# The low part of split weights: a VectorE subtraction, or an adding transfer onto a negated high part

## The chip, the cores and the metric

The kernel runs on one core of a Trainium2 chip. The metric is the device time of one execution in microseconds. Before the change, three timed runs took 3363.51, 3373.67 and 3374.84 us, median 3373.67. One more execution was taken by the hardware profiler; durations below are from it. A core has TensorE (matmuls), VectorE, ScalarE and GpSimd (elementwise work), and SyncE, which only issues transfers. SyncE and GpSimd each have a queue of transfers, issued in program order.

## The reference, cut to what matters

Two stacked blocks on a sequence of 512 positions with 1024 features, all in float32. The first block has two layers; each is a gated feed-forward net, a hybrid mixer (causal attention with a decay, beside a depthwise causal convolution), a second feed-forward net and a gated addition. The second block has four layers of different kinds: a state-space mixer, sliding-window attention, attention over a compressed latent, and a gated unit that mixes positions.

```python
for i in range(DEPTH):                       # first block, 2 layers
    h = h + 0.5 * swiglu(rmsnorm(h, g_ff1[i]), w_ff1_in[i], w_ff1_out[i])
    h = h + hybrid_mixer(rmsnorm(h, g_mix[i]), w_in[i], ...)
    h = h + 0.5 * swiglu(rmsnorm(h, g_ff2[i]), w_ff2_in[i], w_ff2_out[i])
    h = h + sigmoid(rmsnorm(h, g_ple[i]) @ w_ple_gate[i]) * (p[i] @ w_ple_proj[i])
...
for i in range(4):                           # second block: s5, swa, mla, sgu
    x = x + rmsnorm(branch_i(rmsnorm(x, pre_norm[i])), post_norm[i])
```

## The kernel before, in words

Each product of two float32 matrices is done as three matmuls in a reduced-precision float format (`mm3`, L445 to 451). Both operands are split into a high part, the value rounded to that format, and a low part, the value less its high part; the three matmuls are high by high, high by low and low by high, all added up in one PSUM bank.

Weights are packed on the host into units of 8 blocks of 128x128, that is 128x1024 floats or 512 KB. A unit goes through three steps, all called from `block`, by way of `_advance` and `_ahead`:

- `_dma` (L385): SyncE loads the unit from HBM into a `raw` buffer, of which there are 3.
- `_split` (L393): ScalarE casts `raw` to the high part `whi` (L406), and VectorE subtracts it from `raw` to give the low part `wlo` (L407; in the profile its line is L248, that of a helper which records every VectorE operation). `whi` and `wlo` have 3 buffers each.
- the matmuls: eight blocks, three matmuls each.

When the program comes to unit i, it has recorded the split of units up to i+2 and loads for some units more. `self.ui` is then i. There is no scheduler behind that: instructions stand on each engine in the order in which the Python code records them, and each engine works through its own in order. A unit marked `keep` is split into slots of another pool instead; these are the output weights of the four layers of the second block.

The units come in the order of the phases. A first-block layer has 66 units for the first feed-forward net, 52 for the mixer, 66 for the second net and 10 for the gated addition. The second block has 24 units of input weights for the state-space layer (`s5w`), 18 for the sliding window (`swaw`), 33 for the latent attention (`mlaw`), 24 for the gated unit (`sguw`), and 8 kept ones behind each.

GpSimd has other work in the stages that the change touches: scaling rows of attention scores (L1059, L1767), sums of squares (L651), loads of tables for the state-space layer (L1532), loads of a bias table (L1662) and of constants (L1857, L2008). SyncE's queue also carries rearranging copies between partitions, such as those of keys (L951), among the loads of weights.

Of the kernel before, what the change touches and what calls it, by code (L numbers as in the profile page):

```python
# [9 lines left out]
F32R = mybir.dt.float32r  # L10
I32 = mybir.dt.int32
AF = mybir.ActivationFunctionType
ALU = mybir.AluOpType
# [278 lines left out]
class Kern:  # L292
# [84 lines left out]
        return self.vt[:, o + j:o + j + n]  # L377


    def add_units(self, name, keep=False):  # L380
        a = self.t[name]
        for u in range(a.shape[0]):
            self.units.append((a[u], keep))

    def _dma(self):  # L385
        i = self.dmai
# [6 lines left out]
    def _split(self):  # L393
        i = self.spli
        r = self.raws.pop(i)
        if self.units[i][1]:
            hl = self.slots(2), self.slots(2)
            self.kept.append(hl)
        else:
            hl = [[self.wp.tile([P, UB * P], F32, tag=n, name=self.nm(n))] for n in ("whi", "wlo")]  # L400
        self.sps[i] = self.r(hl)
        self.spli += 1
        w = UB * P // len(hl[0])

        def piece(hi, lo, src):
            self.nc.scalar.copy(hi.bitcast(F32R), src)  # L406
            self.v.tensor_tensor(lo.bitcast(F32R), src, hi, op=ALU.subtract)  # L407
        if i == 0:
            a, b = slice(0, w // 2), slice(w // 2, w)
            piece(hl[0][0][:, a], hl[1][0][:, a], r[:, a])  # L410
            return lambda: piece(hl[0][0][:, b], hl[1][0][:, b], r[:, b])
        for j, (hi, lo) in enumerate(zip(*hl)):
            piece(hi, lo, r[:, j * w:(j + 1) * w])
# [1723 lines left out]
def run(tc, t, outT, phases):  # L2137
    with ExitStack() as ctx:
        k = Kern(ctx, tc, t, outT)
        with tc.manual_schedule():  # L2140
            for ph in phases:
                for u in ph[1]:
                    k.add_units(u, ph[0] in ("s5", "swa", "mla", "sgu") and u[-1] == "o")
            k.load()
            k.first(phases[0][2])
            if any(ph[0] in ("s5", "swa") for ph in phases):
                k.aux = Paced(k, k.prepare(), TABLE_RATE)
                if phases[0][0] != "ffn":
                    k.aux.finish()
                    k.aux = None  # L2150
            for i, ph in enumerate(phases):
                nxt = phases[i + 1][2] if i + 1 < len(phases) else (None, 0)
                getattr(k, ph[0])(*ph[3:], nxt)
            if phases[-1][0] != "sgu":
                k.final_out()
# [34 lines left out]
```

## Time and profile before

| | us |
|---|---|
| timed runs, median (lowest to highest) | 3373.67 (3363.51 to 3374.84) |
| profiled execution | 3365.56 |
| its span, first to last instruction | 3363.8 |
| TensorE busy | 3227.5 |
| VectorE busy | 2136.9 |
| ScalarE busy | 1315.8 |
| GpSimd busy | 454.5 |

In the rows below PE is TensorE, PEld its loading of weights, DVE VectorE, ACT ScalarE, POOL GpSimd and SP SyncE. A name such as `wlo<-raw,whi` gives what an instruction writes and reads, without buffer numbers. An arrow in brackets behind a row gives the idle time of the engine before it and what ended that time. Stretches of the span: the first mixer from about 350 to 704 us, the second from about 1480 to 1835, the state-space layer from 2285, the sliding window from 2535, the latent attention from 2770 and the gated unit from 3105 to the end.

### The profile page before, as it was taken

Reading aid. Unit: us, or ns where it says so; the run is one execution under the profiler, and the core shown is the slowest. Engines: PE = TensorE matmul, PEld = TensorE weight load, DVE = VectorE, ACT = ScalarE, POOL = GpSimd, SP = SyncE. Lnnn points to the kernel's source line nnn. Section 1 sums busy time; section 2 is a strip of 40 time slices with the busy share of each in tenths; the row PEclk is TensorE's granted clock in tenths of the full one; section 3 lists DMA queues with packets and bytes.
Section 4 is the critical chain, followed back from the end, with each engine's and each line's share of the span. In section 5 each row is a group of like instructions: output and inputs, shape, how many; then the busy total and the mean of one; then the engine's idle time right before and its main releaser. Section 6 shows DMA issues by size and latency. Waiting matters only on the chain. (4 is left out here: it accounts for less than half of the span.)

```text
span 3363.8 us, 42316 instructions
## 1 busy us (share of the span) xinstructions
PE 3227.5 (96%) x15704; PEld 2704.2 (80%) x15704; DVE 2136.9 (64%) x4128; ACT 1315.8 (39%) x2250; POOL 454.5 (14%) x582
## 2 busy tenths in 40 slices
PE   9999999999999999999999999999999989998997
PEld 7888777788888888887777888887888778787887
DVE  6653488866653676536887654347766766587665
ACT  4322335433322333323444333234334664466433
POOL 0100013001100011000120000010303332044201
PEclk9999999999999999999999999999899989999998
DMA  5433232224432234332322332343732122322221
GB/s 178 137 108 101 88 113 70 92 90 132 139 121 95 94 129 138 114 99 93 99 72 94 104 119 94 106 138 108 257 95 92 63 63 76 110 73 62 86 83 63
DMA packets 122862, 352.27 MB, mean 105 GB/s; under 512 B 31072, under 2 KB 33792, under 8 KB 122656
## 3 DMA queue, kind: packets, MB, share of 16 engines
q1 hardware_dynamic: 106384, 299.88, 28.3%
q0 software_dynamic: 16272, 49.69, 4.4%
q8 instruction: 124, 2.03, 0.2%
q14 instruction: 82, 0.67, 0.1%
HBM read 312.75 MB, written 28.11 MB: 101 GB/s over the span
## 5 line engine op out<-in xcount | busy, mean ns | idle before, releaser
L449 PE MATMUL mm<-s,whi 128*128 128x512 f32 (+1 forms) x3528 | 1382.0, 392 | 20.9 <-DVE s L248 9.1
L451 PE MATMUL mm<-s,wlo 128*128 128x512 f32 (+1 forms) x3528 | 1367.1, 388 | 6.2 <-DVE wlo L248 6.2
L450 PE MATMUL mm<-s,whi 128*128 128x512 f32 (+1 forms) x3528 | 1368.2, 388 | 3.4 <-DVE s L248 3.0
L248 DVE TENSOR_TENSOR wlo<-raw,whi 128x1024 fp32r<-128x1024 f32 (+1 forms) x488 | 594.3, 1224 | 522.9 <-ACT whi L406 519.0
L449 PEld LDWEIGHTS mm<-s,whi 128*128 128x128 f32 x3528 | 667.9, 189 | 153.0 <-ACT s L740 7.4
L451 PEld LDWEIGHTS mm<-s,wlo 128*128 128x128 f32 x3528 | 667.1, 189 | 145.6 <-DVE wlo L248 10.2
L450 PEld LDWEIGHTS mm<-s,whi 128*128 128x128 f32 x3528 | 667.9, 189 | 135.4 <-DVE s L248 8.1
L406 ACT CAST whi<-raw 128x1024 fp32r<-128x1024 f32 (+1 forms) x488 | 508.3, 1046 | 552.1 <-PE mm L450 271.2
L248 DVE TENSOR_TENSOR s<-s,s 128x512 f32<-128x512 f32 (+10 forms) x944 | 471.7, 524 | 170.7 <-ACT s L595 140.7
L248 DVE TENSOR_TENSOR s<-mm,rbc 128x512 f32<-128x512 f32 x296 | 199.4, 685 | 177.7 <-PE mm L451 156.7
L595 ACT CAST s<-s 128x512 fp32r<-128x512 f32 (+1 forms) x213 | 129.9, 616 | 401.2 <-DVE s L248 397.3
L1059 POOL TENSOR_SCALAR s<-s,m 128x128 f32<-128x128 f32 (+3 forms) x128 | 154.5, 1213 | 501.5 <-DVE m L248 388.4
L248 DVE SCALAR_TENSOR_TENSOR s<-s,vecs,s 128x511 f32<-128x511 f32 (+13 forms) x256 | 183.9, 759 | 10.4 <-ACT s L598 6.9
L457 PE MATMUL sd<-s,s 128*128 128x256 f32 (+2 forms) x624 | 125.8, 327 | 40.1 <-DVE s L248 22.8
L457 PEld LDWEIGHTS sd<-s,s 128*128 128x128 f32 x624 | 105.7, 199 | 65.9 <-DVE s L248 33.2
L449 PE MATMUL mm<-s,s 128*128 128x256 f32 x448 | 132.2, 295 | 26.6 <-ACT s L595 22.7
L847 ACT ACTIVATE s<-s 128x512 f32<-128x512 f32 x88 | 55.7, 632 | 253.2 <-DVE s L248 253.2
L740 ACT ACTIVATE s<-h,vecs 128x512 fp32r<-128x512 f32 (+1 forms) x112 | 70.8, 633 | 182.5 <-DVE h L248 182.5
L450 PE MATMUL mm<-s,s 128*128 128x256 f32 x448 | 130.7, 292 | 1.9 <-DVE s L248 1.3
L451 PE MATMUL mm<-s,s 128*128 128x256 f32 x448 | 129.7, 289 | 0.8 <-DVE s L248 0.8
L248 DVE SCALAR_TENSOR_TENSOR s<-h,vecs,s 128x512 fp32r<-128x512 f32 (+1 forms) x112 | 81.2, 728 | 66.9 <-ACT s L740 66.9
L449 PE MATMUL sd<-s,whi 128*128 128x512 f32 x296 | 122.0, 412 | 0.9 <-ACT whi L406 0.9
(213 smaller groups left out, 3264.6 us busy)
## 6 DMA issues: line engine op xcount, KB each, us to landing
raw<-in_mix_dram SPq DMA_DIRECT2D x104, 512.0 KB, 3.5
raw<-in_ff2i_dram SPq DMA_DIRECT2D x88, 512.0 KB, 3.5
raw<-in_ff1i_dram SPq DMA_DIRECT2D x87, 512.0 KB, 3.6
raw<-in_ff1o_dram SPq DMA_DIRECT2D x44, 512.0 KB, 3.5
raw<-in_ff2o_dram SPq DMA_DIRECT2D x44, 512.0 KB, 3.5
raw<-in_mlaw_dram SPq DMA_DIRECT2D x33, 512.0 KB, 3.5
tab<-s POOLq DMA_DIRECT2D x64, 256.0 KB, 2.3
s<-tab POOLq DMA_DIRECT2D x64, 256.0 KB, 6.1
```

Of the source, the lines that this page charges most:

```text
L248: return f(*a, **kw)
L406: self.nc.scalar.copy(hi.bitcast(F32R), src)
L449: mm(ps, wh, xh, start=first, stop=False)
L450: mm(ps, wh, xl, start=False, stop=False)
L451: mm(ps, wl, xh, start=False, stop=last)
L457: self.nc.tensor.matmul(ps, w, x[j], start=first and j == 0, stop=last and j == 1)
L595: nc.scalar.copy(hi.bitcast(F32R), src)
L740: self.nc.scalar.activation(hi.bitcast(F32R), src, AF.Copy, scale=gv)
L847: nc.scalar.activation(sg, ta, AF.Silu)
L1059: nc.gpsimd.tensor_scalar(out=pr[:, c], in0=pr[:, c], scalar1=ri, scalar2=None, op0=ALU.mult)
```

## The change

Units of the mixers and of the second block's input weights get their low part in another way. ScalarE writes the negated, rounded raw weights into `wlo` (an activation with scale -1), and then a transfer on GpSimd's queue, from SBUF to SBUF, adds the raw weights onto it. The sum is again raw less high part. Units of the feed-forward nets and of the gated addition, kept units, and units that are split no more than one ahead of the unit being started (`i > self.ui + 1` is false) still use the subtraction.

```diff
--- before.py
+++ after.py
@@ -377,10 +377,10 @@
         return self.vt[:, o + j:o + j + n]
 
 
-    def add_units(self, name, keep=False):
+    def add_units(self, name, keep=False, summed=False):
         a = self.t[name]
         for u in range(a.shape[0]):
-            self.units.append((a[u], keep))
+            self.units.append((a[u], keep, summed and not keep))
 
     def _dma(self):
         i = self.dmai
@@ -402,9 +402,17 @@
         self.spli += 1
         w = UB * P // len(hl[0])
 
+
+
+        summed = self.units[i][2] and i > self.ui + 1
+
         def piece(hi, lo, src):
             self.nc.scalar.copy(hi.bitcast(F32R), src)
-            self.v.tensor_tensor(lo.bitcast(F32R), src, hi, op=ALU.subtract)
+            if summed:
+                self.nc.scalar.activation(lo.bitcast(F32R), src, AF.Copy, scale=-1.0)
+                self.nc.gpsimd.dma_start(lo, src, accum_op=ALU.add)
+            else:
+                self.v.tensor_tensor(lo.bitcast(F32R), src, hi, op=ALU.subtract)
         if i == 0:
             a, b = slice(0, w // 2), slice(w // 2, w)
             piece(hl[0][0][:, a], hl[1][0][:, a], r[:, a])
@@ -2140,7 +2148,7 @@
         with tc.manual_schedule():
             for ph in phases:
                 for u in ph[1]:
-                    k.add_units(u, ph[0] in ("s5", "swa", "mla", "sgu") and u[-1] == "o")
+                    k.add_units(u, ph[0] in ("s5", "swa", "mla", "sgu") and u[-1] == "o", ph[0] not in ("ffn", "ple"))
             k.load()
             k.first(phases[0][2])
             if any(ph[0] in ("s5", "swa") for ph in phases):
```

In the order of instructions 188 low parts move. On ScalarE, at the end of the first mixer, where casts of weights stand among casts of the mixer's own tiles (`raw` is a loaded unit, `s` a slot), before:

```order
L406 CAST whi_5367<-raw_5244 128x1024
L1007 CAST s_5385<-s_4911 128x512
L1007 CAST s_5404<-s_4949 128x512
L406 CAST whi_5411<-raw_5290 128x1024
L1007 CAST s_5429<-s_4988 128x512
L1007 CAST s_5448<-s_5026 128x512
L406 CAST whi_5455<-raw_5328 128x1024
```

And now:

```order
L410 CAST whi_5409<-raw_5284 128x1024
L412 ACTIVATE wlo_5410<-raw_5284 128x1024
L1015 CAST s_5428<-s_4943 128x512
L1015 CAST s_5447<-s_4982 128x512
L410 CAST whi_5454<-raw_5331 128x1024
L412 ACTIVATE wlo_5455<-raw_5331 128x1024
L1015 CAST s_5473<-s_5022 128x512
L1015 CAST s_5492<-s_5061 128x512
L410 CAST whi_5499<-raw_5370 128x1024
```

Lines in the changed file are 4 or 8 higher. Each cast of a unit is followed by a second pass over the same raw tile, and the mixer's casts stand behind both.

On GpSimd, in the sliding-window layer, where the bias table is loaded into slots and sums of squares follow, before:

```order
L1662 DMA s_19873<-bias_d 128x2x256
L1662 DMA s_19874<-bias_d 128x2x256
L1662 DMA s_19875<-bias_d 128x2x256
L1662 DMA s_19876<-bias_d 128x2x256
L651 TENSOR_TENSOR s_19736<-s_19736,s_19991 128x256
L651 TENSOR_TENSOR s_19736<-s_19736,s_19998 128x256
```

And now:

```order
L1670 DMA s_19994<-bias_d 128x2x256
L1670 DMA s_19995<-bias_d 128x2x256
L1670 DMA s_19996<-bias_d 128x2x256
L1670 DMA s_19997<-bias_d 128x2x256
L413 DMA wlo_20022<-raw_19562 128x1024
L659 TENSOR_TENSOR s_19857<-s_19857,s_20113 128x256
L659 TENSOR_TENSOR s_19857<-s_19857,s_20120 128x256
```

The adding transfer stands behind the last bias load and ahead of the sums. It waits for ScalarE's second pass, and so do the sums behind it.

## Rows read from the trace of the kernel before

**Rows 1.** Page head and section 1: busy time, share and instructions of each engine

```profile
span 3363.8 us, 42316 instructions
PE 3227.5 (96%) x15704; PEld 2704.2 (80%) x15704; DVE 2136.9 (64%) x4128; ACT 1315.8 (39%) x2250; POOL 454.5 (14%) x582
```

**Rows 2.** Stretches: length, busy of PE, PEld, DVE, ACT, POOL, clock, DMA, GB/s

```profile
350.00:704.00 354.00, 332.57 (x1492) 269.85 (x1491) 266.32 (x511) 147.73 (x244) 43.97 (x38) 0.98 0.29 88
704.00:1065.00 361.00, 360.59 (x1628) 298.75 (x1627) 213.99 (x381) 119.17 (x160) 29.75 (x56) 1.00 0.37 121
2535.00:2770.00 235.00, 206.68 (x1249) 183.09 (x1248) 166.97 (x454) 131.20 (x373) 83.15 (x97) 0.94 0.20 66
```

**Rows 3.** Waits of TensorE: us in total, times, longest us

```profile
PE sd L457 <- DVE s L248: 22.8, 22, 4.3
PE mm L449 <- DVE s L248: 10.5, 9, 2.1
```

**Rows 4.** Page section 5: costliest groups, the weight split

```profile
L248 DVE TENSOR_TENSOR wlo<-raw,whi 128x1024 fp32r<-128x1024 f32 (+1 forms) x488 | 594.3, 1224 | 522.9 <-ACT whi L406 519.0
L406 ACT CAST whi<-raw 128x1024 fp32r<-128x1024 f32 (+1 forms) x488 | 508.3, 1046 | 552.1 <-PE mm L450 271.2
```

**Rows 5.** Transfers: queue's share; issues, count, size, us to landing

```profile
q1 hardware_dynamic: 106384, 299.88, 28.3%
raw<-in_mix_dram SPq DMA_DIRECT2D x104, 512.0 KB, 3.5
s<-in_wsT_dram POOLq DMA_DIRECT2D x4, 256.0 KB, 4.6
tab<-s POOLq DMA_DIRECT2D x64, 256.0 KB, 2.3
bias_d<-bias POOLq DMA_DIRECT2D x1, 3072.0 KB, 14.6
```

**Rows 6.** Timeline, undisturbed stretch: start, us, engine, instruction, idle before

```profile
595.66 1.05 ACT L406 CAST whi<-raw 128x1024 fp32r<-128x1024 f32 x1 [1.13 <-PE mm L450]
607.02 0.39 PE L451 MATMUL mm<-s,wlo 128*128 128x512 f32 x1
```

**Rows 7.** Timeline, first mixer: late splits and VectorE's chain

```profile
404.12 1.98 ACT L406 CAST whi<-raw 128x1024 fp32r<-128x1024 f32 x2
407.34 0.50 PE L451 MATMUL mm<-s,wlo 128*128 128x512 f32 x1 [1.40 <-DVE wlo L248]
675.58 1.23 DVE L248 TENSOR_TENSOR wlo<-raw,whi 128x1024 fp32r<-128x1024 f32 x1 [1.64 <-ACT whi L406]
712.87 1.04 ACT L406 CAST whi<-raw 128x1024 fp32r<-128x1024 f32 x1
716.73 0.39 PE L451 MATMUL mm<-s,wlo 128*128 128x512 f32 x1
```

**Rows 8.** Timeline, start of the state-space stage

```profile
2303.91 1.04 ACT L406 CAST whi<-raw 128x1024 fp32r<-128x1024 f32 x1
2306.26 0.50 PE L451 MATMUL mm<-s,wlo 128*128 128x512 f32 x1 [0.53 <-DVE wlo L248]
```

**Rows 9.** Timeline, last late split, in the gating stage

```profile
3277.89 1.04 ACT L406 CAST whi<-raw 128x1024 fp32r<-128x1024 f32 x1
3282.46 0.39 PE L451 MATMUL mm<-s,wlo 128*128 128x512 f32 x1
```

**Rows 10.** Timeline, sliding-window stage, GpSimd's bias loads

```profile
2564.59 5.04 POOL L1662 DMA_DIRECT2D s<-bias_d  x7
2569.09 0.28 PE L451 MATMUL mm<-s,wlo 128*128 128x256 f32 x1
```

**Rows 11.** Timeline, first mixer, SyncE's queue and the cast before

```profile
436.46 1.05 ACT L406 CAST whi<-raw 128x1024 fp32r<-128x1024 f32 x1
439.12 0.33 SPq L389 DMA_DIRECT2D raw<-in_mix_dram  x1
441.68 2.50 SPq L951 DMA_DIRECT2D s<-s  x4
```

## The prediction

> **What bounds the kernel now.** I read the busy shares first, then the busy time by stage, then who waits for whom on TensorE, and last the timelines around the weight splits. TensorE is busy in 3227.5 of 3363.8 us [rows 1], so an edit on another engine counts only where it makes TensorE start earlier or later. The stages differ [rows 2]: in the feed-forward stretch TensorE is busy 360.59 of 361 us, in the first mixer 332.57 of 354 (the second is its like), in the sliding-window stage 206.68 of 235 at a granted clock of 0.94. The change leaves the feed-forward and gate weights as they are, so all that it can win lies in the stages that have gaps.
>
> What ends those gaps: 22.8 us of waits for VectorE results before the attention products and 10.5 us before projections [rows 3]. That is the part that a less loaded VectorE could shorten, 33.3 us in all.
>
> What stands against it is how early a weight unit is split. In the undisturbed stretch a unit's high part is cast as soon as TensorE has let go of its buffer: the cast at 595.66 was released by a matmul and ended at 596.71, and the first matmul on this unit's low part (the third of its first block) starts at 607.02 [rows 6]. That is 10.3 us from the cast's end to the first use, two units' worth of matmuls. I call this the margin. Before, one VectorE subtraction of 1.22 us had to fit in it.
>
> **The change part by part.** The order shows 188 low parts that leave VectorE, 188 activations that come to ScalarE and 188 transfers that come to GpSimd's queue. Per unit:
>
> VectorE loses 1224 ns, 188 x 1.224 = 230 us. It also loses the wait for the cast ahead of it: 519 us over 488 units, 1.06 us each [rows 4]. Since VectorE works in order, whatever stood behind a subtraction moves up by up to 2.3 us.
>
> ScalarE gains one pass over 128x1024. The trace has no such activation; the nearest row is the cast of the same tile, 1046 ns [rows 4]. Ends: half and twice the cast, 0.5 and 2.1 us; I take the row, 1.05. 188 of them are 197 us, beside other work on an engine busy 39% [rows 1], except that they push the landing back by 1.05.
>
> GpSimd's queue gains a transfer that waits for the activation, and stands in order among its other work. No adding transfer is in the trace. The rows nearest to it [rows 5]: 512 KB from HBM on SyncE's queue land 3.5 us after issue, 256 KB loads on GpSimd's queue in 4.6, stores of 256 KB in 2.3, 3 MB in 14.6. The add must read the destination besides the source; one more pass over 0.524 MB costs what the hardware queue shows, 28.3% of 3363.8 us for 299.88 MB, that is 1.66 us. 3.5 + 1.66 = 5.2; from the 4.6 us row with half a pass more, 5.4. With a slower start on GpSimd I take 5.6 us from issue to the moment TensorE may start, ends 2.3 and 14.6.
>
> The Trainium skill, Collectives: The Full Stack (The bandwidth ceiling), says that an add in the transfer engines is slow because it needs two source reads, so it runs at about half the rate of a copy; by a plain copy's 3.5 us instead the stalls below would be some 27 us and not 63. No run here shows which holds. The Trainium skill, DMA: Bandwidth & Descriptors (Anatomy of one DMA), gives 2.0 us plus bytes over 436e3 for GpSimd's path, an estimate of 3.2 us for a plain copy of this size; the 4.6 us row for half the size is longer, so I hold to the rows.
>
> So a low part is ready 1.05 + 5.6 = 6.65 us after the cast's end, where it was 1.3 to 2.5 us. With the full margin of 10.3 us this is hidden. It is not where the cast itself comes late, behind other ScalarE work. About 40 of the 188 units have less than 6.65 us: the first is the one at 404 us in rows 7, the last has its cast end at 3278.93 and its use at 3282.46 [rows 9]. A stall delays all that follows, so within a run of units only what a stall has not already covered counts.
>
> Mixers. Cast ends 405.1 (half of the pair), low part used at 407.34, where TensorE already waits 1.40 us: margin 2.2, late by 4.4. At the end of the stage, cast end 713.91, use 716.73: late by 3.8; the next unit, worked likewise, 2.5. Together 10.7 a mixer, 21.4 for two [rows 7]. Between them the units from 651 to 695 us have margins down to 1.3, but there VectorE sets the pace: each subtraction is preceded by 1.64 us of idle and takes 1.23 [rows 7], and with both gone the chain is faster than TensorE. I count these at nothing; uncovered they would be 9 us a mixer.
>
> State-space stage. Cast end 2304.95, use 2306.26: margin 1.3, late by 5.3 [rows 8]. The next unit has the same margin and gets 2.3 us back from VectorE: 3.0. Four more casts late by 1 to 5 us, worked the same way, give 7.5, the largest at the output weights. One transfer stands behind eight table loads in GpSimd's queue: 2.6. Sum 18.4.
>
> Queue places. In the sliding-window stage the transfer stands behind the eight bias loads; seven of them hold GpSimd until 2569.63, and the low part is used at 2569.09 [rows 10]: 5.6 + 0.5 = 6.1, more if their data goes first. Three such places in the last two stages, worked the same way: 2.1, 3.6 and 5.8. Sum 17.6. Scattered late casts in those stages, the one of rows 9 (6.65 - 3.5 = 3.1) the largest: 5.4.
>
> Stalls so far: 21.4 + 18.4 + 17.6 + 5.4 = 63 us.
>
> SyncE's queue. A raw buffer is given back when the transfer has read it, no longer when VectorE has. At 439.12 SyncE issues a load that waited for a subtraction, behind it stand four copies that rearrange keys, issued at 441.68 [rows 11], and TensorE waits for these. The unit's cast ends at 437.51; with 6.65 us the load goes out at 444.2 and the copies 2.7 us later than now. Two mixers: 5 us.
>
> Clock. In the sliding-window stage 28 us of gaps go with a granted clock of 0.94 over 235 us, a mean of the 2.4 GHz level (1.00, as in the feed-forward row) and the 1.2 GHz one [rows 2]: 14 us of clock; part of it lies in the gaps. At a sixth of a microsecond for each of stall: +10, ends 0 and 35.
>
> Given back. Of the 33.3 us in rows 3 I take 18, because some of those VectorE results hang on ScalarE, which now has more to do; ends 0 and 33.
>
> Sum: 63 + 5 + 10 - 18 = +60 us. The profiled execution took 3365.56 us, 1.8 more than its span and 8 below the median of 3373.67 of the timed runs; 3365.6 + 60 = 3426.
>
> **The rivals.**
> VectorE wins (faster). The transfer lands in 3 us, near the 2.3 us stores of rows 5, and the 33.3 us all go. Stalls then: 6 in the mixers, 6 in the state-space stage, 8 at the queue places, 20 in all; the gaps that go give some 7 us of clock back: 20 - 33 - 7 = -20, 3345 us. For it: the subtractions sit in front of exactly the work that TensorE waits for. Against it: places where TensorE already waits for a low part at all [rows 7, 8].
>
> It cancels. Landing 4.5 us: stalls 44, clock 5, given back 33: +15, 3381 us.
>
> The transfer engines set the pace (much slower). If the add lands after more than 10.3 - 1.05 = 9.2 us, then the full margin fails too, and every unit is late. Three buffers turn, so an excess is shared by three units. At 12 us: 2.8 / 3 x some 70 units of the undisturbed kind = 65; the fourteen places above get 6.4 more each, 90; with 63, the clock at 40 and 18 given back, +240, 3605 us. For it: nothing in the trace shows the rate of an add, and per unit there are one load and one add on the same 16 engines, every 5.5 us (rows 6: two units in some 11). Against it: at 1.66 us a pass, three passes fit.
>
> **How the numbers follow.** Forecast 0.45, VectorE wins 0.20, cancels 0.17, transfer engines set the pace 0.18. The forecast's own range, landing 4.8 to 7 us, is 3390 to 3500. The range to 8 in 10 reaches to 3340, which takes in most of the faster case, and to 3570, which leaves out about half of the slowest. Half a per cent, 17 us, is about what a measurement of this kernel can tell from no change. Faster than that 0.20; within it 0.20 (the cancelling case and the forecast's lower edge); slower 0.60.
>
> **What would show it.** In the new profile: the adding transfer's row with a landing of 5 to 7 us; TensorE waiting for a transfer into the low part, 50 to 80 us in about 15 to 30 waits, the longest at the mixers' starts, at the start of the state-space stage and behind the bias loads; none in the stretch around 600 us; subtractions down to about 300; casts that come one after another with a second pass of 1.05 us. The waits for VectorE of rows 3 down by about half. I am wrong if waits for the low part stay under 25 us, or if they appear in the stretch with full margin.

## The result and the profile after

The changed kernel is slower: 3486.56 us, median of four runs (3484.02 to 3487.33), against 3368.64 us for the kernel before in four runs (3363.51 to 3374.84). The ratio is 1.0348, 95% interval 1.0324 to 1.0372. The profiled execution's span grew from 3363.8 us [rows 1] to 3482.2, by 118.4 us. The forecast was +60, 3426 us: the sign was right, the size half.

Page head and section 1 of the profile after:

```profile
span 3482.2 us, 42664 instructions
PE 3257.8 (94%) x15704; PEld 2726.0 (78%) x15704; DVE 1917.9 (55%) x3940; ACT 1493.2 (43%) x2438; POOL 607.8 (17%) x770
```

Two parts can be read off at once. TensorE is busy 30.3 us longer over as many matmuls, 15,704 (3257.8 less the 3227.5 of [rows 1]), and it idles 224.4 us where it idled 136.3, 88.1 more. VectorE's busy time fell by 219 us, ScalarE's rose by 177.

Where it went by stage shows in the windows after. The columns are those of [rows 2]. They hold, but for one at an edge, the matmuls of the first mixer, of the feed-forward nets and the gated addition behind it, and of the state-space stage:

```profile
350.19:723.98 373.79, 336.31 (x1492) 272.16 (x1491) 215.46 (x464) 191.56 (x290) 80.85 (x82) 0.95 0.62 147
723.98:1504.63 780.65, 776.86 (x3492) 642.46 (x3491) 451.57 (x802) 257.25 (x344) 66.20 (x123) 1.00 0.38 120
2333.07:2608.53 275.46, 242.29 (x1244) 206.82 (x1243) 144.32 (x228) 116.77 (x167) 64.73 (x98) 0.91 0.68 184
```

The stretches of before that [rows 2] does not have:

```profile
704.00:1480.00 776.00, 774.85 (x3491) 641.18 (x3490) 455.20 (x805) 254.52 (x341) 62.69 (x118) 1.00 0.36 118
2285.00:2535.00 250.00, 237.95 (x1243) 204.93 (x1242) 173.80 (x250) 95.42 (x145) 45.86 (x76) 0.93 0.50 158
```

The first mixer takes 20 us more, the state-space stage 25, the latent attention 24 (335.00 to 359.21). The feed-forward stretch, whose weights the change leaves alone, takes 5 more. The granted clock fell in both mixers and in all four stages of the second block, in the first mixer from 0.98 to 0.95, and stayed at 1.00, the 2.4 GHz level, in the feed-forward stretch, where TensorE idles for less than 4 of 781 us.

TensorE's waits after, the ones that answer to [rows 3] and the new ones (lines are 8 higher, so the L457 and L449 of before are L465 and L457 here, and L451 is L459):

```profile
PE mm L459 <- DMA wlo<-raw: 56.9, 19, 6.3
PE sd L465 <- DMA s<-s: 36.9, 6, 8.7
PE sd L465 <- DVE s L248: 18.1, 19, 4.3
PE mm L457 <- DVE s L248: 11.1, 7, 4.0
PE sd L457 <- issue: 7.3, 1, 7.3
PE sd L457 <- DMA s<-s: 6.3, 2, 3.5
```

Two waits rule. The low part, now written by a transfer, is late 19 times in the projections. And the copies that rearrange keys between partitions (`s<-s`), which the change does not touch, are late for 36.9 + 6.3 us. For the 7.3 us, which fall in the latent attention, the profile names no releaser (`issue`). Four such copies are issued there 5.5 us before the wait ends, behind a load; the quickest lands 5.4 us after its issue, and the wait falls below 2 us in the runs below that issue loads later or take the adds around the copies out. So I count it with them.

The two new groups beside those of [rows 4], and the transfers that answer to [rows 5]. Of the subtractions 300 are left, of 1220 ns each:

```profile
L413 POOL DMA_DIRECT2D wlo<-raw x188 | 163.1, 871 | 1201.0 <-ACT wlo L412 1104.3
L412 ACT ACTIVATE wlo<-raw 128x1024 fp32r<-128x1024 f32 x188 | 198.3, 1055 | 0.0
q0 software_dynamic: 43344, 148.27, 19.8%
wlo<-raw POOLq DMA_DIRECT2D x188, 512.0 KB, 5.2
```

The second pass takes 1055 ns and follows the cast without a gap. The add lands 5.2 us after issue (median).

**The late low parts.** Timeline after, where the first mixer starts ([rows 7]), at the start of the state-space stage ([rows 8]) and behind the bias loads of the sliding window ([rows 10]):

```profile
411.48 0.79 PE L459 MATMUL mm<-s,wlo 128*128 128x512 f32 x1 [5.53 <-DMA wlo<-raw]
...
2358.77 0.80 PE L459 MATMUL mm<-s,wlo 128*128 128x512 f32 x1 [5.06 <-DMA wlo<-raw]
...
2649.04 0.58 PE L459 MATMUL mm<-s,wlo 128*128 128x256 f32 x1 [6.29 <-DMA wlo<-raw]
```

TensorE waits 5.53, 5.06 and 6.29 us there, and each wait ends where the add lands. What such a wait costs besides shows in two short windows behind the first one, after and, from the same matmul on, before (columns as above; the clock is the third last):

```profile
411.50:414.50 3.00, 3.00 (x7) 2.42 (x8) 1.91 (x3) 1.76 (x3) 0.85 (x1) 0.50 0.99 205
```

```profile
407.40:410.00 2.60, 2.60 (x12) 2.14 (x13) 2.50 (x4) 0.94 (x2) 0.00 (x0) 1.00 0.63 187
```

After the 5.53 us gap the granted clock is 0.50, the 1.2 GHz level, and TensorE starts 7 matmuls in 3.0 us; before, behind its 1.40 us, it is 1.00 and starts 12 in 2.6.

**The key copies.** First mixer after, SyncE's queue, TensorE at its two waits, and ScalarE and GpSimd ahead of the second (the kernel before is in [rows 11]):

```profile
449.68 0.33 SPq L389 DMA_DIRECT2D raw<-in_mix_dram  x1
450.10 3.90 SPq L959 DMA_DIRECT2D s<-s  x4
455.00 0.55 PE L465 MATMUL sd<-s,s 128*128 128x256 f32 x1 [7.79 <-DMA s<-s]
...
468.75 1.05 ACT L412 ACTIVATE wlo<-raw 128x1024 fp32r<-128x1024 f32 x1
471.06 1.45 POOL L1067 TENSOR_SCALAR s<-s,m 128x256 f32<-128x256 f32 x1 [5.67 <-DVE m L248]
472.46 0.91 POOL L413 DMA_DIRECT2D wlo<-raw  x1
477.07 0.33 SPq L389 DMA_DIRECT2D raw<-in_mix_dram  x1
477.50 2.39 SPq L959 DMA_DIRECT2D s<-s  x4
482.41 1.15 PE L465 MATMUL sd<-s,s 128*128 128x256 f32 x2 [8.69 <-DMA s<-s]
```

Read it from the third line from the end backwards. The load at 477.07 writes a raw buffer that the add of 472.46 still reads, so it goes out when that has landed. The copies stand right behind the load in SyncE's queue. The add itself was ready when the pass ended at 469.80, but GpSimd works in order and stood at a scaling of attention scores that waited for VectorE until 471.06. A second thing comes on top: the copies go out together with a load, beside adds on the same transfer engines, and take longer. From issue to landing, all 32 copies of the two mixers, before and after (L951 and L959 are the same line of code):

```profile
DMA to landing us min/median/max: 2.2/2.3/3.7
```

```profile
DMA to landing us min/median/max: 4.6/6.2/8.5
```

The profile of before hides part of what these waits were. TensorE's two long waits for copies in the first mixer before, and the one of the second mixer that answers to the second of them:

```profile
444.07 0.55 PE L457 MATMUL sd<-s,s 128*128 128x256 f32 x1 [2.88 <-DMA s<-s]
465.35 0.55 PE L457 MATMUL sd<-s,s 128*128 128x256 f32 x1 [4.27 <-ACT whi L406]
1615.82 0.55 PE L457 MATMUL sd<-s,s 128*128 128x256 f32 x1 [4.40 <-DMA s<-s]
```

The 4.27 us are put down to a cast of weights, which this matmul does not read; a key copy issued at 463.03 landed at 465.2, and that cast ended at 465.3. The like wait of the second mixer is put down to the copies. The same holds for 1.34 us in the latent attention, at the matmul that waits 7.3 us after. In the account I count both with the copies.

**The account**, from all of TensorE's waits of the two profiles:

| term | before | after | change | forecast |
|---|---|---|---|---|
| waits for low parts, from VectorE or a transfer | 9.0 | 63.8 | +54.8 | +63 |
| waits for key copies (with the 7.3 us, and the 4.27 and 1.34 of before) | 17.0 | 50.5 | +33.5 | +5 |
| waits for VectorE's other results and for high parts | 55.8 | 44.2 | -11.6 | -18 |
| waits for ScalarE's other results and GpSimd's | 43.2 | 54.2 | +11.0 | 0 |
| TensorE busy longer at the lower clock | 3227.5 | 3257.8 | +30.3 | +10 |
| sum | | | +118.0 | +60 |

### The profile page after: what moved, and what is told of

It is laid out like the page before. It is cut to its first block, busy times and chain, and to the rows that moved or that the text cites. A ratio compares the mean times of both kernels' runs of the same rounds, so it can differ in the third digit from the quotient of the medians.

```text
span 3482.2 us, 42664 instructions
## 1 busy us (share of the span) xinstructions
PE 3257.8 (94%) x15704; PEld 2726.0 (78%) x15704; DVE 1917.9 (55%) x3940; ACT 1493.2 (43%) x2438; POOL 607.8 (17%) x770
## 3 DMA queue, kind: packets, MB, share of 16 engines
q0 software_dynamic: 43344, 148.27, 19.8%
## 5 line engine op out<-in xcount | busy, mean ns | idle before, releaser
L459 PE MATMUL mm<-s,wlo 128*128 128x512 f32 (+1 forms) x3528 | 1380.8, 391 | 59.2 <-DMA wlo<-raw 56.9
L457 PE MATMUL mm<-s,whi 128*128 128x512 f32 (+1 forms) x3528 | 1393.7, 395 | 23.4 <-DVE s L248 11.1
L459 PEld LDWEIGHTS mm<-s,wlo 128*128 128x128 f32 x3528 | 674.9, 191 | 207.5 <-DMA wlo<-raw 66.5
L457 PEld LDWEIGHTS mm<-s,whi 128*128 128x128 f32 x3528 | 676.5, 192 | 155.7 <-DVE s L248 8.9
L458 PEld LDWEIGHTS mm<-s,whi 128*128 128x128 f32 x3528 | 676.4, 192 | 132.8 <-DVE s L248 3.5
L248 DVE TENSOR_TENSOR wlo<-raw,whi 128x1024 fp32r<-128x1024 f32 (+1 forms) x300 | 363.6, 1220 | 460.3 <-ACT whi L410 457.9
L413 POOL DMA_DIRECT2D wlo<-raw x188 | 163.1, 871 | 1201.0 <-ACT wlo L412 1104.3
L412 ACT ACTIVATE wlo<-raw 128x1024 fp32r<-128x1024 f32 x188 | 198.3, 1055 | 0.0
L465 PE MATMUL sd<-s,s 128*128 128x256 f32 (+2 forms) x624 | 125.2, 326 | 62.9 <-DMA s<-s 36.9
L465 PEld LDWEIGHTS sd<-s,s 128*128 128x128 f32 x624 | 104.9, 198 | 88.5 <-issue 39.6
L457 PE MATMUL mm<-s,s 128*128 128x256 f32 x448 | 132.8, 296 | 25.6 <-ACT s L603 21.7
L248 DVE TENSOR_TENSOR s<-sd,s 128x512 fp32r<-128x512 f32 (+3 forms) x186 | 93.9, 528 | 71.5 <-DMA ud<-s 19.1
L458 PE MATMUL mm<-s,s 128*128 128x256 f32 x448 | 131.1, 293 | 2.2 <-DVE s L248 1.7
```

The lines of the kernel that those rows point to most:

```text
L248: return f(*a, **kw)
L412: self.nc.scalar.activation(lo.bitcast(F32R), src, AF.Copy, scale=-1.0)
L413: self.nc.gpsimd.dma_start(lo, src, accum_op=ALU.add)
L457: mm(ps, wh, xh, start=first, stop=False)
L458: mm(ps, wh, xl, start=False, stop=False)
L459: mm(ps, wl, xh, start=False, stop=last)
```

## The experiments

Theory A: the time goes to late low parts and to key copies behind loads that wait for adds, each with the clock it costs; elsewhere the change is free or a small relief. Rival B: the extra passes and transfers cost by themselves, wherever they stand. Medians below are set against the kernel before on the same chip (3370.33, 3368.43 and 3371.06 us in the three sets of runs). The expectations go by the profile's rows as they name the releasers: 11 us of waits for copies before, and 39 more after.

### Loads issued one unit later, in the changed kernel and in the kernel before

```diff
-        while self.dmai <= min(i + self.RAW_AHEAD - hold, self.spli + 2, n - 1):
+        while self.dmai <= min(i + self.RAW_AHEAD - hold, self.spli + 1, n - 1):
```

A load is then recorded one unit later, behind copies that it stood ahead of, and waits for the add of an older unit. The second run makes the same edit in the kernel before.

> The changed kernel, with weight loads recorded one unit later, so that a load in SyncE's queue waits for the add of an older unit and not of the newest. Theory A (of the 118 us that the change cost, low parts that come late are 55 of TensorE's idle time, key copies that stand behind such a load in SyncE's queue and share the transfer engines with it and with the add are 39, and the clock that is lost with the idle time is 30): the waits for key copies fall from 43 to about 20 us, those for the low part stay near 57, the time falls from 3487 to about 3455. Theory B (the second passes on ScalarE and the longer queue of GpSimd delay the attention stages; the key copies are only where it shows): no change, 3482 to 3492.

> Control: the kernel before with the same later loads. Theory A: loads there wait only for a subtraction, the waits for key copies are 11 us and fall by 3 at most; 3362 to 3372 against 3369. Theory B says the same. Much faster than that would mean that the later loads help for a reason of their own.

The changed kernel came to 3452.29 us, 1.0241 [1.0225, 1.0256], 34 us less than without the edit. The kernel before came to 3367.38, 0.9989 [0.9979, 0.9998], so the edit alone is worth some 3 us. Waits for the copies and for low parts in the changed kernel, and the copies' landing:

```profile
PE mm L459 <- DMA wlo<-raw: 65.0, 21, 7.6
PE sd L465 <- DMA s<-s: 15.0, 4, 4.3
```

```profile
DMA to landing us min/median/max: 2.3/2.8/6.8
```

The copies land in 2.8 us instead of 6.2, and TensorE's waits for them, counted as in the account, fall by 32 us (50.5 to 18.4; 2.0 and 1.3 of it stand in other rows). The low parts stay late: 73.1 us in all their rows, 9 more than in the changed kernel. So the loads that wait for adds ahead of the copies in SyncE's queue are the cause of the second term.

### The low part without its transfer

```diff
                 self.nc.scalar.activation(lo.bitcast(F32R), src, AF.Copy, scale=-1.0)
-                self.nc.gpsimd.dma_start(lo, src, accum_op=ALU.add)
```

> The changed kernel without the adding transfer: the low part of the 188 units is left as the negated high part. ScalarE's second passes and VectorE's relief stay, transfers and their waits go. Theory A: waits for the low part under 5 us, waits for key copies near 12 as before the change, time 3352 to 3372. Theory B: ScalarE's passes alone cost, 3400 to 3440.

It came to 3348.93 us, 0.9936 [0.9921, 0.995]: 21 us under the kernel before, a little below what A expected, and far from B. The 188 passes on ScalarE are all there:

```profile
PE 3222.8 (96%) x15704; PEld 2704.2 (81%) x15704; DVE 1915.3 (57%) x3940; ACT 1492.8 (45%) x2438; POOL 447.6 (13%) x582
```

The passes do not look free: TensorE's waits for other results of ScalarE and GpSimd are 51.0 us here against 43.2 before. But VectorE's relief outweighs them, and 21 us is what is left when no transfer has to be waited for. I take that as about the most that this change could win; no run shows a bound.

### The second pass kept, then subtracted as before

```diff
             self.nc.scalar.copy(hi.bitcast(F32R), src)
+            if summed:
+                self.nc.scalar.activation(lo.bitcast(F32R), src, AF.Copy, scale=-1.0)
             self.v.tensor_tensor(lo.bitcast(F32R), src, hi, op=ALU.subtract)
```

This is the kernel before with the extra pass, whose result the subtraction overwrites.

> The kernel before with one pass more on ScalarE: for the same 188 units it writes the negated weights into the low part's buffer, and VectorE's subtraction overwrites them. No transfer, no relief of VectorE, 188 passes of 1.05 us. Theory A: the pass costs little, 3372 to 3390. Theory B: 3405 to 3440.

3433.82 us, 1.0188 [1.0171, 1.0205]. A missed by more than 40 us, and the time lies within B's range. What happened is in VectorE's row:

```profile
L248 DVE TENSOR_TENSOR wlo<-raw,whi 128x1024 fp32r<-128x1024 f32 (+1 forms) x488 | 594.5, 1223 | 611.9 <-ACT whi L410 415.3 <-ACT wlo L412 193.5
```

and in TensorE's waits for other VectorE results:

```profile
PE mm L455 <- DVE s L248: 22.5, 13, 4.0
```

The subtraction now waits for the pass, 193.5 us in all, and VectorE, which works in order, holds back its own other results; the wait of the second row was 10.5 us in [rows 3]. I had overlooked that when I wrote the expectation. So this kernel mixes the pass with a VectorE that stands behind it. The run without the transfer has the same passes and no such wait (and 188 subtractions fewer), and is faster than before. From the two together I read that here the wait costs and not the pass by itself, but no run separates them. The run is no evidence for A; against B speak the run without the transfer and those below.

### Subtraction kept where the low part is late, around the key copies, and in both

```diff
-        summed = self.units[i][2] and i > self.ui + 1
+        summed = self.units[i][2] and i > self.ui + 1 and i not in self.LATE
```

LATE holds the 32 units whose casts end too close to the first use, COPIES the 35 units split around the key copies of the two mixers and the latent attention (`not in self.COPIES`), and the third kernel leaves out both sets (`not in self.LATE | self.COPIES`), so that 121 adds remain.

> The changed kernel, but 32 of the 188 units, those whose cast comes late, keep the subtraction. Theory A: waits for the low part fall from 57 to under 12 us, waits for key copies stay near 43, the lost clock falls with the idle time: 3412 to 3430. Theory B: the waits for the low part are replaced by others, 3460 to 3480.

> The changed kernel, but the 35 units that are split while key copies are on their way (10 in each mixer, 15 in the latent attention) keep the subtraction. Theory A: waits for key copies fall from 43 to about 12 us, waits for the low part stay near 57: 3438 to 3452. Theory B: those units are a fifth of the passes and transfers, so a fifth of the cost goes: 3460 to 3470.

> The changed kernel with both sets of units, 67 less those counted twice, on the subtraction; the other adds stay. Theory A: waits for low part and key copies near those before the change, the rest of VectorE's relief stays: 3362 to 3385, perhaps as fast as the kernel before. Theory B: over 120 of 188 passes and transfers stay, so over half of the cost does: 3430 to 3450.

| adds left | median | ratio to before | less than the changed kernel |
|---|---|---|---|
| 188 less the late ones, 156 | 3421.17 | 1.0154 [1.0136, 1.0172] | 65.4 |
| 188 less those around copies, 153 | 3443.92 | 1.022 [1.0197, 1.0244] | 42.6 |
| less both, 121 | 3376.20 | 1.0022 [1.0013, 1.0032] | 110.4 |

Copies and low parts in TensorE's waits, with the late units subtracted, then with those around the copies, then with both:

```profile
PE sd L467 <- DMA s<-s: 39.5, 4, 11.0
PE mm L461 <- DMA wlo<-raw: 13.2, 7, 5.8
```

```profile
PE mm L460 <- DMA wlo<-raw: 58.4, 19, 6.6
PE sd L466 <- DMA s<-s: 10.9, 6, 4.4
```

```profile
PE sd L468 <- DMA s<-s: 11.5, 7, 4.4
PE mm L462 <- DMA wlo<-raw: 7.8, 5, 4.2
```

Counted as in the account, the waits for copies are 52.1, 16.6 and 17.6 us in the three kernels. Each set takes away its own term and leaves the other: two causes, nearly additive, 65.4 + 42.6 = 108.0 against 110.4. The wait without a named releaser is gone in the second and third kernel. With both, 121 adds remain and the time is 7.8 us above the kernel before: on chosen units the adds cost almost nothing, which B does not allow, but bring nothing either.

### A plain copy in place of the add

```diff
-                self.nc.gpsimd.dma_start(lo, src, accum_op=ALU.add)
+                self.nc.gpsimd.dma_start(lo, src)
```

> The changed kernel with a plain copy in the place of the adding transfer: the low part of the 188 units is the raw weights. Same bytes written, same waits, but the destination isn't read. If an add costs two passes: landing falls from 5.2 to about 3.7 us, packets of 4 KB on that queue from some 330 ns to 170; on theory A the waits for the low part then fall from 57 to about 33 us and for key copies to about 30, time 3440 to 3460. If the fixed part of a transfer is what counts: landing 4.8 to 5.2 and 3475 to 3490.

3423.40 us, 1.016 [1.0145, 1.0175], lower than the 3440 to 3460 expected, with landing and waits near those expected:

```profile
q0 software_dynamic: 43344, 148.27, 11.7%
wlo<-raw POOLq DMA_DIRECT2D x188, 512.0 KB, 3.3
```

```profile
PE mm L459 <- DMA wlo<-raw: 34.7, 12, 5.8
PE sd L465 <- DMA s<-s: 25.7, 5, 7.0
```

The same 148.27 MB and the same packets occupy the transfer engines for 11.7% of 3421.3 us, 400 us, against 19.8% of 3482.2 us, 689 us, with the add. Less the 148 us of this queue before the change (4.4% of 3363.8, 49.69 MB), the 188 transfers take 252 and 541 us, 1.34 and 2.88 us each: an add costs 2.15 times a copy there. In landing it is 5.2 against 3.3 us, and in the kernel's time 63 us, more than half of what the change lost. Both terms shrink, since the loads wait for the landing too.

### Both sets subtracted, and loads issued later

> The 121 adds of the run with both sets subtracted, and in addition the loads issued one unit later, so that SyncE waits less. A (the adds cost only where they are late or hold copies up; elsewhere they relieve VectorE): waits of TensorE for the copies of keys fall from 11.5 us to about 7, low-part waits stay at 8 to 12; the gain of later loads in the kernel before was 2 to 4 us, so 3367 to 3377 against 3368 of before: no version with the adding transfer is clearly faster than before. B (the passes and transfers themselves cost, wherever they stand): 121 of 188 of the cost remain, so as in the run with both sets it stays above 3400. If it comes under 3358, the relief of VectorE is worth more than I count.

3371.78 us, 1.0006 [0.9996, 1.0016]: as expected, no different from the kernel before. Low parts and copies after:

```profile
PE mm L462 <- DMA wlo<-raw: 15.3, 7, 5.2
PE sd L468 <- DMA s<-s: 7.2, 6, 2.9
```

The copies' row is 4.3 us below that of the run with both sets only because the profile puts one more such wait down to a cast; counted as in the account it is 16.4 us against 17.6. No version with the adding transfer was found that beats the kernel before. A deeper lookahead, which would give every low part more time, was not tried.

## Why the prediction was half right

**What bounds the kernel** held. The stretch with the full margin has no wait for a low part (in 560 to 710 us the profile after lists only waits for VectorE, 5.4 us), though adds and loads keep the transfer engines busy 66% of it. In the main both sides of the margin came out as argued.

**VectorE and ScalarE** held: 230 us off the one were forecast, and the subtractions fell from 594.3 to 363.6; a pass was put at 1.05 us and takes 1055 ns.

**The transfer** held: 5.6 us were taken from ends of 2.3 and 14.6, 5.2 measured. The Trainium skill, Collectives: The Full Stack (The bandwidth ceiling), gives half the rate of a copy to ReduceScatter, because its add needs two source reads. For an add within this core the runs agree on the ratio, 2.15 times a copy on the transfer engines; that the second read is the reason no run shows. The estimate of 3.2 us for a plain copy, worked out from the Trainium skill, DMA: Bandwidth & Descriptors (Anatomy of one DMA), agrees as well, with 3.3 measured. I was right to charge the add a second pass, but setting that estimate aside because of the 4.6 us row was wrong: that row is a load from HBM, and a copy of twice its size within SBUF landed 1.3 us sooner.

**Stalls on late low parts** held in the sum and at the largest places: first mixer's start 5.53 us (4.4 more than the 1.40 it already waited, 5.8), state-space start 5.06 (0.53 + 5.3), bias loads 6.29 (6.1). Not every place held. The gating stage's unit of [rows 9] waited 0.36 us where 3.1 was forecast, and the longest wait of that stage is at another unit, behind loads of constants in GpSimd's queue:

```profile
3265.53 0.58 PE L459 MATMUL mm<-s,wlo 128*128 128x256 f32 x1 [5.61 <-DMA wlo<-raw]
3399.70 0.50 PE L459 MATMUL mm<-s,wlo 128*128 128x512 f32 x1 [0.36 <-DMA wlo<-raw]
```

The three queue places forecast at 2.1, 3.6 and 5.8 us waited 3.44, 5.61 and 0.25. So there is some luck in a sum of 54.8 us against 63. The run with the late units subtracted shows that they cost 65 us, clock included.

**SyncE's queue** is the step that failed: "the copies 2.7 us later than now. Two mixers: 5 us" was 33.5. The mechanism was named and its place was right, but the term was sized at one place with one delay. TensorE waits for two groups of copies in each mixer and again for copies in the latent attention; I had counted one group per mixer and none in the latent attention. And at each place the later issue is only part of the delay. At the one that I had worked out the copies are issued 2.9 us after TensorE began to wait, before 0.5, so 2.4 us later and close to the 2.7; but from their issue to TensorE's start it is 4.9 us against 2.4 (450.10 to 455.00, 441.68 to 444.07). I had put the longer landing in company at nothing. At the second group GpSimd also holds the add behind work that waits for VectorE (2.7 us at 469.80). The run with loads one unit later and the run with subtraction around the copies both take this term out, by 32 and 34 us of waits.

**Clock** was mis-sized: 10 us forecast, 30.3 measured, for 88 us more of idle time, a third of a microsecond for each. The row that I read (28 us of gaps with 14 us of clock, [rows 2]) said a half, and I cut it to a sixth on the argument that part of it lies in the gaps. Other runs lie between a third and about a half: without the transfer, 10.4 us less idle and 4.7 less busy; with pass and subtraction, where no transfer is added, 45.3 more idle and 22.9 more busy.

**Given back** was too high: 11.6 us against 18, and only 4.1 of it stands in the two rows named (33.3 to 29.2), where half was expected; the rest is in smaller rows. Against it stand 11.0 us of later results of ScalarE and GpSimd, which I costed at nothing.

Key copies +28.5, clock +20.3, ScalarE and GpSimd +11.0, less given back +6.4, low parts -8.2: together the 58 us that were missing.

**The rivals.** That VectorE wins fails on the landing; yet its gain is real, 21 us in the run without a transfer. That it cancels fails on the landing too, 5.2 us against 4.5, and on the 33 us to be given back. That the transfer engines set the pace fails: the median add lands in 5.2 us, within the 9.2 that the margin leaves, and there is no wait where the margin is full.

## What to carry to other kernels

When a step is handed to something that finishes later, follow not only who reads its result but what its end gives back: here a raw buffer, whose load stood in an in-order queue ahead of copies that nobody had touched. Count every place where that happens, and give small transfers the landing they have in company, not alone. Idle time on TensorE was charged again in clock in every run above that had clearly more of it; take the ratio from the row that shows both, and don't discount it without a reason from a trace. And where a wait is put down to an instruction whose result the waiting one does not read, look for what else ended at that moment.

## What the runs showed of the hardware that was not expected

- An add between SBUF tiles occupied the transfer engines 2.15 times as long as a copy of the same bytes (2.88 against 1.34 us for 512 KB), and GpSimd's issue of it took 871 ns on average where the copy's took 541:

```profile
L413 POOL DMA_DIRECT2D wlo<-raw x188 | 101.8, 541 | 1220.6 <-ACT wlo L412 1122.7
```

- The mixers' key copies of 128 KB each, issued in fours, landed in 2.3 us (median) in the kernel before, where the load ahead of them had gone out earlier. They took 6.2 when released together with a load beside adds, and 4.9 with a load beside plain copies.
- The clock's price: 0.34 to 0.52 us more (or less) of busy TensorE for each us of idle time more (or less), in the seven kernels above whose idle time differs from the kernel before by over 10 us. All run the same matmuls.
